# Differential q and k and the forgetting attention's gate with h's two halves as one 512-column stream

## The chip, the cores and the metric

The kernel runs on one core of one Trainium2 chip. The metric is the device time of one execution in microseconds (us). The kernel before took 937.58 us, the median of three runs (937.49 to 937.73). TensorE is called PE, VectorE DVE, ScalarE ACT, GpSimd POOL and SyncE, which starts the transfers of weights, SP.

## The reference, cut to what matters

Two layers of a streaming encoder on 256 rows of 1024 values. Each layer normalises its input to `h` and multiplies it by one wide matrix whose columns feed three branches: a forgetting attention (q, k, v, a gate `fg`), a state-space scan, and a differential attention (`dq`, `dk`, `dv`, a gate `dg`). Only these parts bear on the change:

```python
h = rmsnorm(x, norm_w)
proj = jnp.einsum('bld,de->ble', h, w_in)
(fq, fk, fv, ff, fg, sz, sxbc, sdt, dq, dk, dv, dg, mg) = jnp.split(proj, split_points, axis=-1)
...
y_a = o_a.transpose(0, 2, 1, 3).reshape(bsz, L, BRANCH_W) * jax.nn.silu(fg)
...
q = partial_rope(dq.reshape(bsz, L, DIFF_HEADS, 2, DIFF_HD), cos, sin).transpose(0, 2, 3, 1, 4)
k = partial_rope(dk.reshape(bsz, L, DIFF_HEADS, 2, DIFF_HD), cos, sin).transpose(0, 2, 3, 1, 4)
```

## The kernel before, in words

The precision is near float32, reached with fp32r matmuls: each operand is split into a high half (rounded to fp32r) and a low half (the rest), and of the four products three are summed, high by high, high by low and low by high.

**Weights.** They come in blocks of 512 columns, 34 to a layer, each in four units of 128 x 1024 (`load_chunk`). SP loads a unit (`raw`, four buffers), ACT casts it to the high half `whi` (L231), DVE subtracts to get the low half `wlo` (L232). Eight buffers of each kind hold two blocks.

**Two kinds of block.** In a B block (`bform`, L249) a piece of h is stationary and 512 columns of weights stream. In an A block (`aform`, L264) the weights are stationary and h, transposed, streams: 256 columns of its high or its low half. An A block has two halves of 48 matmuls, and each half fills one PSUM bank with two pieces of 128 outputs side by side. 14 blocks of a layer are A blocks: fq0, fk0, fg0, fq1, fk1, fg1 of the forgetting attention, four of the scan (sB, sC, sx0, sx1), and dq0, dk0, dq1, dk1 of the differential attention. Three banks (`pp`) take the sums of all blocks, three (`pq`) the small matmuls, two (`pt`) the transposes.

**h.** `make_h` normalises 128 rows at a time (`tt` is 0 or 1). `split_rows` transposes four pieces of 128 x 128 into one bank (L198), and `split_bank` takes them out two at a time: ACT copies the high half (L188), DVE subtracts for the low half (L189). The halves are four tiles each of 128 x 2 x 256; `at` picks one piece.

**What follows an A block.** `g_evac` (the gate): ACT takes a tanh from the bank and DVE makes the product, 512 columns each. `r_evac` (differential q and k): ACT copies 512 columns out (L792); the rotary step follows. `t_evac` (forgetting q and k) calls `split_q` or `split_k`, whose copies (L389, L394) and subtracts (L392) empty the bank.

**Beside the blocks** the attentions run as jobs: `scores` multiplies q by k (L406, L408) into a `pq` bank; DVE adds the mask and bias in one step (L411), ACT takes exponentials (L415). The bias of the forgetting attention reaches DVE by way of memory: `sc_cum` (L368, L369) is written to `scr` and read back as `sc`, and POOL masks it (L435).

**Order.** Each engine works in its own order, fixed ahead of the run by a list scheduler that the program uses; instructions with `URGENT` priority go first where they can. At the start a few weight casts are held behind h: the casts of the first block's units 1 to 3 are issued after the last copy and subtract of h's first 128 rows (`after=` in `load_chunk`), and its matmuls go by units (`EARLY`).

Of the kernel before, what the change touches and what calls it, by code (L numbers as in the profile page):

```python
# [24 lines left out]
KT = D // P  # L25
UNITS = 4
KU = KT // UNITS
# [69 lines left out]
def trunk(ctx: ExitStack, tc: tile.TileContext, x, norm_w, weights, small, vectors,  # L97
          final_norm_w, rope_t, out):
    nc = tc.nc
    V, S, G, PE = nc.vector, nc.scalar, nc.gpsimd, nc.tensor  # L100
# [6 lines left out]
    tp = ctx.enter_context(tc.tile_pool(name="tp", bufs=2))  # L107
    sm = ctx.enter_context(tc.tile_pool(name="sm", bufs=2))
    dr = ctx.enter_context(tc.tile_pool(name="dr", bufs=1, space=bass.MemoryType.DRAM))
    pp = ctx.enter_context(tc.tile_pool(name="pp", bufs=3, space=bass.MemoryType.PSUM))  # L110
    pq = ctx.enter_context(tc.tile_pool(name="pq", bufs=3, space=bass.MemoryType.PSUM))
    pt = ctx.enter_context(tc.tile_pool(name="pt", bufs=2, space=bass.MemoryType.PSUM))
# [3 lines left out]
    def a2(shape=None, dtype=F32):  # L116
        return ap.tile(shape or [P, 2, 256], dtype, name="a2")

    def rows():
        return [a2([P, 512]) for _ in range(2)]  # L120

    def halves():
        return tuple([a2(dtype=F32R) for _ in range(4)] for _ in range(2))

    def at(half, kt):
        return half[kt // 2][:, kt % 2, :]

    def bank(pool, name):
        return pool.tile([P, 512], F32, name=name)

    ident = const.tile([P, P], F32, name="ident")
# [47 lines left out]
    def rstd_of(ss, n, eps, width):  # L179
        r = sm.tile([P, 8], F32, name="rstd")  # L180
        V.tensor_scalar(out=r[:, 0:width], in0=ss, scalar1=1.0 / n, scalar2=eps,  # L181
                        op0=ALU.mult, op1=ALU.add)
        G.tensor_tensor(out=r[:, 0:width], in0=r[:, 0:width], in1=mhalf[:, 0:width], op=ALU.pow)  # L183
        return r

    def split_bank(ps, hi, lo, scale=None):
        if scale is None:
            return (S.copy(out=hi, in_=ps),  # L188
                    V.tensor_tensor(out=lo, in0=ps, in1=hi.bitcast(F32), op=ALU.subtract))  # L189
        else:  # L190
            S.activation(out=hi, in_=ps, func=AF.Copy, scale=scale)
            V.scalar_tensor_tensor(out=lo, in0=ps, scalar=scale, in1=hi.bitcast(F32),
                                   op0=ALU.mult, op1=ALU.subtract)

    def split_rows(src, hi, lo, tt, c):
        ps = bank(pt, "pt")
        for j in range(4):
            PE.transpose(ps[:, j * P:(j + 1) * P], src[:, j * P:(j + 1) * P], ident)  # L198
        ts = slice(tt * P, (tt + 1) * P)
        p4 = ps.rearrange("p (i j t) -> p i j t", i=2, t=P)  # L200
        for i in range(2):
            last = split_bank(p4[:, i], hi[2 * c + i][:, :, ts], lo[2 * c + i][:, :, ts])
        return last

    def norm_scale(ss):
        V.tensor_reduce(out=ss[:, 0:1], in_=ss, axis=AX.X, op=ALU.add)
        return rstd_of(ss[:, 0:1], D, EPS, 1)

    def norm_apply(xt, xs, r, wb, c):
        V.scalar_tensor_tensor(out=xs[c], in0=xt[c], scalar=r[:, 0:1], in1=wb[c],  # L210
                               op0=ALU.mult, op1=ALU.mult)

    chunks, _ = chunk_list()
# [39 lines left out]
    def aform(ch, act, jj):  # L253
        units, n = ch
        ahi, alo = act
        ps = bank(pp, "pp")
        for u in range(UNITS):
            whi, wlo = units[u]
            for k in range(KU):
                kt = u * KU + k  # L260
                for j in range(2):
                    c0 = (2 * jj + j) * P
                    for i, (w, a) in enumerate(((whi, ahi), (whi, alo), (wlo, ahi))):
                        PE.matmul(ps[:, j * T:(j + 1) * T], lhsT=w[:, k, c0:c0 + P], rhs=at(a, kt),  # L264
                                  start=(kt == 0 and j == 0 and i == 0), stop=(kt == KT - 1 and j == 1 and i == 2))
        return ps

    scr_x = dr.tile([2, P, D], F32, name="scr_x")
    L = [dict() for _ in range(DEPTH)]

    def make_h(l, tt, xt, xs, ss, gap):
        st = L[l]
        if tt == 0:
            st["hT"] = halves()
        with tc.high_priority(URGENT):
            r = norm_scale(ss)
            for c in range(2):
                norm_apply(xt, xs, r, st["nwb"], c)
        yield gap
        with tc.high_priority(URGENT):  # L280
            for c in range(2):
                st["split"] = split_rows(xs[c], st["hT"][0], st["hT"][1], tt, c)
        st[f"h{tt}"] = True

    def load_nwb(l):
# [11 lines left out]
    def start_job(gen, *args):  # L297
        jobs.append([gen(*args), slot[0]])
# [444 lines left out]
    def plan(l):  # L743
        st = L[l]
# [41 lines left out]
            return f  # L786

        def r_evac(key):
            def f(jj, ps):
                t = a2()  # L790
                st.setdefault("_" + key, []).append(t)
                S.copy(out=t, in_=ps.rearrange("p (a t) -> p a t", t=T))  # L792
                if jj == 1 and key[:2] == "dk":
                    start_job(rope, l, int(key[2]))
            return f

        def g_evac(key):
            def f(jj, ps):
                t = a2()
                p3 = ps.rearrange("p (a t) -> p a t", t=T)  # L800
                S.activation(out=t, in_=p3, func=AF.Tanh, scale=0.5)
                V.scalar_tensor_tensor(out=t, in0=t, scalar=1.0, in1=p3, op0=ALU.add, op1=ALU.mult)
                st[f"{key[0:2]}{2 * int(key[2]) + jj}"] = t
            return f

        def c_evac(key, j0):
            def f(jj, ps):
# [124 lines left out]
        for c in range(2):  # L932
            B(f"sz{c}", [gate_evac("sz", 512 * c, c == 1)])
        A("dq0", r_evac("dq0"), pre=start(diff))
        A("dk0", r_evac("dk0"))
        for c in range(2):
# [31 lines left out]
    def prefetch(n, after=None, behind=()):  # L968
        while queue and n > 0:
            l_, k_, _, off, m = queue.pop(0)  # L970
            loaded.append((l_, k_, load_chunk(off, m, after, behind)))
            n -= 1
# [16 lines left out]
    for tt in range(2):  # L989
        xs, ss = rows(), sm.tile([P, 4], F32, name="ss")  # L990
        with tc.high_priority(URGENT):
            for q in range(4):
                qs = slice(256 * (q % 2), 256 * (q % 2) + 256)
                a, b = xs[q // 2][:, qs], xt[tt][q // 2][:, qs]
                if q < ACTSQ[tt]:
                    S.activation(out=a, in_=b, func=AF.Square, accum_out=ss[:, q:q + 1])
                else:
                    V.tensor_tensor_reduce(out=a, in0=b, in1=b, scale=1.0,
                                           scalar=0.0, op0=ALU.mult, op1=ALU.add, accum_out=ss[:, q:q + 1])
        g = make_h(0, tt, xt[tt], xs, ss, 1)  # L1000
# [8 lines left out]
    for idx, it in enumerate(items):  # L1009
        if it["key"] == "dq0" and it["l"] == 0:  # L1010
            with tc.issue_after(L[0]["split"][0].ins), tc.issue_after(L[0]["split"][1].ins):
                load_params(1)
            nc.sync.dma_start(rot, rope_t)
        if it["pre"]:
            it["pre"]()
        l = it["l"]
        if it["wait"]:
            n = 0
            while it["wait"] not in L[l]:
                assert jobs  # L1020
                pump(100.0)
                n += 1
            if n > 1:
                print("forced", l, it["key"], n)
        prefetch(it["n"])
        got = [loaded.pop(0) for _ in range(it["n"])]
        assert got[0][:2] == (l, it["key"]), (got[0][:2], it["key"])
        if idx == 0:
            ch, act = got[0][2], it["act"]()
            it["evac"][0](0, bform(ch, act, 0, EARLY))  # L1030
            while "h1" not in L[0]:
                pump(BUDGET)
            it["evac"][0](1, bform(ch, act, 1))
            pump(BUDGET)
            got, it["evac"] = got[1:], it["evac"][1:]
            with tc.issue_after(L[0]["split"][0].ins), tc.issue_after(L[0]["split"][1].ins):
                load_params(0)
        for tt, pieces in enumerate(it.get("final", ())):
            while f"mT{tt}" not in L[l]:
                pump(100.0)  # L1040
            for c0, c1 in pieces:
                ps = bform(got[c0 // 512][2], it["act"](), tt, c0=c0 % 512, c1=c0 % 512 + c1 - c0)
                it["evac"](tt, c0, c1)(ps)
                pump(BUDGET)
        for s in range(0 if "final" in it else 2):
            for (_, _, ch), ev in zip(got, it["evac"]):
                if it["kind"] == "A":
                    ev(s, aform(ch, it["act"](), s))
                else:
                    while f"{it['flag']}{s}" not in L[l]:  # L1050
                        pump(100.0)
                    ev(s, bform(ch, it["act"](), s))
                pump(BUDGET)
# [27 lines left out]
```

## Time and profile before

| | |
|---|---|
| median of three runs | 937.58 us |
| profiled execution, its own time | 938.8 us |
| its span, first to last instruction | 937.1 us |
| PE busy | 924.8 us (99%) |
| DVE busy | 705.0 us (75%) |
| ACT busy | 588.0 us (63%) |
| mean granted clock of PE | 0.994 |

Busy is the time in which at least one instruction of the engine ran. Matmuls overlap in the profile: the time of a step is the distance from one start to the next, and a mean of 384 ns for a matmul is not its step. A timeline row gives its start, the time up to its last end, and in brackets the idle time of the engine ahead of it with what ended that.

### The profile page before, as it was taken

To read this page: it belongs to the slowest core of one execution; us is meant where nothing else is said; L and a number is where in the kernel's file an instruction comes from. 1 tells how busy PE (TensorE), PEld (TensorE's weight loads), DVE (VectorE), ACT (ScalarE), POOL (GpSimd) and SP (SyncE) were. 2 spreads that over 40 slices of the span, in tenths; PEclk is the share of its full clock that TensorE was granted. 3 is DMA by queue.
4 is the path that set the end of the run, shared out by engine and by line. 5 is a ranking of instruction groups with operands and counts; after the bars stand their busy time and mean duration, and the time that the engine had idled before them with its cause. 6 is when DMAs were issued, how large, how long until landed. Compare 5 with 4: busy or idle time off the path is not lost.

```text
span 937.1 us, 16550 instructions
## 1 busy us (share of the span) xinstructions
PE 924.8 (99%) x6012; PEld 828.5 (88%) x6012; DVE 705.0 (75%) x1472; ACT 588.0 (63%) x1115; POOL 56.9 (6%) x135
## 2 busy tenths in 40 slices
PE   7999999999999999999999999999999999999997
PEld 5999999988898988888889999998889899888886
DVE  5688888989667868764768789789877686787474
ACT  4668776655567768554546779666545695885441
POOL 2001200000010001100010111000001000010000
PEclk7999999999999999999999999999999999999999
DMA  6866735674555655555557674356646465554551
GB/s 227 266 214 209 222 102 169 206 241 137 179 184 175 191 173 180 175 157 198 191 174 258 222 225 151 125 180 207 209 150 199 155 203 174 189 180 153 186 179 45
DMA packets 60321, 172.48 MB, mean 184 GB/s; under 512 B 7312, under 2 KB 15824, under 8 KB 60240
## 3 DMA queue, kind: packets, MB, share of 16 engines
q1 hardware_dynamic: 59952, 170.91, 55.6%
q8 instruction: 47, 0.77, 0.3%
q10 hardware_dynamic: 288, 0.52, 0.1%
q14 instruction: 34, 0.28, 0.1%
HBM read 167.14 MB, written 2.16 MB: 181 GB/s over the span
## 4 chain that ended last, share of the span: by engine, by line
PE 96%; DMA 2%; DVE 1%; ACT 0%; SPq 0%; issue 0%; POOLq 0%; POOL 0%
PE pp L249 52%; PE pp L264 33%; PE pq L406 1%; PE pq L408 1%; PE pt L470 1%; PE pq L455 1%; PE pq L607 1%; DMA raw<-in_weights_dram 1%; PE pt L654 1%; PE pt L198 1%; PE pq L718 1%; PE pq L617 0%; DMA sc<-scr 0%; DMA scr<-sc_cum 0%; PE pt L549 0%; PE pt L725 0%
## 5 line engine op out<-in xcount | busy, mean ns | idle before, releaser
L249 PE MATMUL pp<-whi,a 128*128 128x512 f32 (+2 forms) x1488 | 452.6, 384 | 2.0 <-ACT a L188 1.2
L232 DVE TENSOR_TENSOR wlo<-raw,whi 128x1024 fp32r<-128x1024 f32 (+1 forms) x296 | 350.1, 1195 | 81.4 <-ACT whi L231 78.4
L231 ACT CAST whi<-raw 128x1024 fp32r<-128x1024 f32 (+1 forms) x296 | 301.9, 1028 | 126.6 <-PE pp L249 69.3
L264 PE MATMUL pp<-a,whi 128*128 128x256 f32 x1792 | 332.5, 284 | 0.0
L249 PEld LDWEIGHTS pp<-whi,a 128*128 128x128 f32 x1488 | 275.2, 189 | 55.4 <-ACT a L188 1.7
L249 PE MATMUL pp<-wlo,a 128*128 128x512 f32 (+2 forms) x744 | 282.9, 382 | 0.0
L264 PEld LDWEIGHTS pp<-a,whi 128*128 128x128 f32 x1792 | 281.2, 191 | 1.6 <-issue 0.9
L264 PE MATMUL pp<-a,wlo 128*128 128x256 f32 x896 | 254.7, 284 | 0.0
L264 PEld LDWEIGHTS pp<-a,wlo 128*128 128x128 f32 x896 | 171.2, 191 | 0.6 <-issue 0.2
L249 PEld LDWEIGHTS pp<-wlo,a 128*128 128x128 f32 x744 | 140.4, 189 | 25.8 <-DVE wlo L232 0.5
L494 DVE SCALAR_TENSOR_TENSOR a<-sw,pT,a 128x255 f32<-128x255 f32 (+2 forms) x96 | 42.0, 477 | 9.4 <-ACT a L491 9.2
L183 POOL TENSOR_TENSOR rstd<-rstd,mhalf 128x2 f32<-128x2 f32 (+2 forms) x24 | 18.5, 773 | 462.7 <-DVE rstd L181 462.7
L835 DVE SCALAR_TENSOR_TENSOR a<-a,pp 128x512 f32<-128x512 f32 x24 | 16.4, 683 | 22.3 <-PE pp L249 22.3
L188 ACT CAST a<-pt 128x256 fp32r<-128x256 f32 x32 | 11.5, 371 | 33.2 <-PE pt L198 26.4
L415 ACT ACTIVATE sc<-sc,nm 128x128 f32<-128x128 f32 (+1 forms) x64 | 28.5, 447 | 5.9 <-DVE nm L411 5.6
L391 POOL MEMSET a<- 64x256 f32 x64 | 18.8, 317 | 184.4 <-PE pq L408 80.9
L415 ACT ACTIVATE sc<-sc,dnm 128x128 f32<-128x128 f32 (+1 forms) x64 | 28.5, 449 | 0.6 <-DVE dnm L411 0.4
L406 PE MATMUL pq<-a,a 128*128 128x256 f32 (+1 forms) x128 | 27.0, 267 | 0.3 <-DVE nm L411 0.3
L435 POOL TENSOR_SCALAR_AFFINE_SELECT sc<-sc 128x256 f32<-128x256 f32 x32 | 16.3, 510 | 151.3 <-DMA sc<-scr 129.1
L411 DVE CUSTOM_DVE_ANT_0 sc<-pq,bmask 128x128 f32<-128x128 f32 (+1 forms) x64 | 20.2, 350 | 4.5 <-PE pq L408 4.5
L810 ACT COPY sw<-pp 128x512 f32<-128x512 f32 x16 | 9.3, 581 | 22.6 <-PE pp L264 17.0
L411 DVE CUSTOM_DVE_ANT_0 sc<-pq,sc 128x128 f32<-128x128 f32 (+1 forms) x64 | 19.7, 350 | 4.7 <-POOL sc L435 4.5
(168 smaller groups left out, 831.0 us busy)
## 6 DMA issues: line engine op xcount, KB each, us to landing
raw<-in_weights_dram SPq DMA_DIRECT2D x280, 512.0 KB, 4.5
raw<-in_weights_dram SPq DMA_DIRECT2D x16, 272.0 KB, 3.5
sc<-scr SPq DMA_DIRECT2D x16, 256.0 KB, 5.3
a<-scr SPq DMA_DIRECT2D x16, 256.0 KB, 6.1
a<-in_x_dram SPq DMA_DIRECT2D x8, 256.0 KB, 5.7
sc<-scr SPq DMA_DIRECT2D x16, 128.0 KB, 4.9
a<-in_norm_w_dram SPq DMA_DIRECT2D x4, 256.0 KB, 6.6
rp<-a SPq DMA_DIRECT2D x32, 32.0 KB, 3.2
```

Of the source, the lines that this page charges most:

```text
L183: G.tensor_tensor(out=r[:, 0:width], in0=r[:, 0:width], in1=mhalf[:, 0:width], op=ALU.pow)
L231: S.copy(out=hi, in_=raw)
L232: V.tensor_tensor(out=lo, in0=raw, in1=hi.bitcast(F32), op=ALU.subtract)
L249: PE.matmul(ps[:, 0:(c1 or n) - c0], lhsT=at(a, kt)[:, ts], rhs=w[:, k, c0:c1 or n], start=((u, k, i) == order[0]), stop=((u, k, i) == ord ...
L264: PE.matmul(ps[:, j * T:(j + 1) * T], lhsT=w[:, k, c0:c0 + P], rhs=at(a, kt), start=(kt == 0 and j == 0 and i == 0), stop=(kt == KT - 1 an ...
L391: G.memset(low[j][rest, i, :].bitcast(F32), 0.0)
L406: PE.matmul(ps[:, i * n:(i + 1) * n], lhsT=q[i][:, j, qs], rhs=k[i][:, j, 0:n], start=(i == 0), stop=False)
L411: V.tensor_tensor_reduce(out=sc[:, i, sl], in0=ps[:, i * n:(i + 1) * n], in1=bias(i)[:, sl], scale=-0.125, scalar=BIG, op0=ALU.add, op1=AL ...
L415: S.activation(out=sc[:, i, sl], in_=sc[:, i, sl], func=AF.Exp, scale=-1.0, bias=nm[:, i, t:t + 1], accum_out=rs[:, i, t:t + 1])
L435: G.affine_select(out=v, in_=v, pattern=[[0, 2], [-1, P]], compare_op=ALU.is_ge, fill=NEG, base=0, channel_multiplier=1)
L494: V.scalar_tensor_tensor(out=xc[:, s:T], in0=u[:, 0:T - s], scalar=pr["conv"](j, k), in1=xc[:, s:T], op0=ALU.mult, op1=ALU.add)
L835: V.scalar_tensor_tensor(out=t, in0=t, scalar=1.0, in1=ps, op0=ALU.add, op1=ALU.mult)
```

## The change

h is now eight tiles of 128 x 2 x 256, one for each 128 of the 1024 inputs: the high half in the first 256 columns, the low half behind it. `split_h` takes the place of `split_rows` for h and takes out one transposed piece at a time, as the two halves of a piece lie in one tile and two pieces don't. For fg0, fg1, dq0, dq1, dk0 and dk1 `wide_form` takes the place of `aform`: for each piece of 128 outputs, the high weights meet both halves of h in one matmul of 512 columns, and the low weights meet the high half in one of 256, which adds to the left half of the bank. A bank so holds one piece of 128 outputs, not two, and `folded` adds its two halves (an ACT copy of the right one, a DVE addition of the left) into a tile in SBUF ahead of what `g_evac` and `r_evac` did with the bank.

```diff
     def at(half, kt):
-        return half[kt // 2][:, kt % 2, :]
+        return half[kt] if len(half) == KT else half[kt // 2][:, kt % 2, :]
+
+    def side_by_side():
+        both = [a2(dtype=F32R) for _ in range(KT)]
+        return both, tuple([t[:, s, :] for t in both] for s in range(2))
...
+    def split_h(src, both, tt, c):
+        ps = bank(pt, "pt")
+        for j in range(4):
+            PE.transpose(ps[:, j * P:(j + 1) * P], src[:, j * P:(j + 1) * P], ident)
+        ts = slice(tt * P, (tt + 1) * P)
+        for j in range(4):
+            h = both[4 * c + j]
+            last = split_bank(ps[:, j * P:(j + 1) * P], h[:, 0, ts], h[:, 1, ts])
+        return last
...
+    def wide_form(ch, both, j):
+        units, n = ch
+        ps = bank(pp, "pp")
+        for u in range(UNITS):
+            whi, wlo = units[u]
+            for k in range(KU):
+                kt, cols = u * KU + k, slice(j * P, (j + 1) * P)
+                PE.matmul(ps, lhsT=whi[:, k, cols], rhs=both[kt], start=(kt == 0), stop=False)
+                PE.matmul(ps[:, 0:T], lhsT=wlo[:, k, cols], rhs=both[kt][:, 0, :],
+                          start=False, stop=(kt == KT - 1))
+        return ps
+
+    def folded(f, new):
+        pair = []
+
+        def g(j, ps):
+            if j % 2 == 0:
+                pair.append(new())
+            d = pair[-1][:, j % 2, :]
+            S.copy(out=d, in_=ps[:, T:2 * T])
+            V.tensor_tensor(out=d, in0=ps[:, 0:T], in1=d, op=ALU.add)
+            if j % 2:
+                f(j // 2, pair[-1])
+        return g
...
         def r_evac(key):
-            def f(jj, ps):
-                t = a2()
+            def f(jj, t):
                 st.setdefault("_" + key, []).append(t)
-                S.copy(out=t, in_=ps.rearrange("p (a t) -> p a t", t=T))
                 if jj == 1 and key[:2] == "dk":
                     start_job(rope, l, int(key[2]))
-            return f
+            return folded(f, a2)
...
                 if it["kind"] == "A":
-                    ev(s, aform(ch, it["act"](), s))
+                    if it["key"][:2] in ("dq", "dk", "fg"):
+                        for j in (2 * s, 2 * s + 1):
+                            ev(j, wide_form(ch, L[l]["both"], j))
+                    else:
+                        ev(s, aform(ch, it["act"](), s))
```

`g_evac` is wrapped in `folded` in the same way, with a scratch tile `sw`; its tanh and product then read that tile.

The scheduler sets a new order with the new instructions. ACT at the start, before: the cast of unit 0 of the first block, the copies of h's first 128 rows (`a_149` to `a_152`, two pieces each), two casts, then the squares for the second 128 rows.

```order
L231 CAST whi<-raw 128x1024 [waits DMAHW4_49]
L188 CAST a_149<-pt 128x2x128 [waits PE_49]
L188 CAST a_150<-pt 128x2x128 [waits DVE_49]
L188 CAST a_151<-pt 128x2x128 [waits PE_49]
L188 CAST a_152<-pt 128x2x128 [waits DVE_49]
L231 CAST whi<-raw 128x1024 [waits DMAHW5_49]
L231 CAST whi<-raw 128x1024 [waits DMAHW0_49]
L996 ACTIVATE a_229,ss<-a_107 128x256 [waits DMAHW6_49]
```

The same place on ACT now, from the fourth of eight copies of h (`a_149` to `a_156`, one piece each) on:

```order
L192 CAST a_152<-pt 128x128 [waits DVE_49]
L192 CAST a_153<-pt 128x128 [waits PE_49]
L192 CAST a_154<-pt 128x128 [waits DVE_49]
L192 CAST a_155<-pt 128x128 [waits DVE_49]
L192 CAST a_156<-pt 128x128 [waits DVE_49]
L1032 ACTIVATE a_237,ss<-a_107 128x256 [waits DMAHW6_49]
L1032 ACTIVATE a_237,ss<-a_107 128x256
L1032 ACTIVATE a_238,ss<-a_108 128x256 [waits DMAHW7_49]
L1032 ACTIVATE a_238,ss<-a_108 128x256
L245 CAST whi<-raw 128x1024 [waits DMAHW5_49]
```

The four squares (L1032, formerly L996) moved ahead of the cast of unit 1. PE in block fg0 of layer 0, before, where the scores (`pq`) stand among fg0's narrow matmuls; `a_149` and `a_153` are the two halves of h's first two pieces:

```order
L264 MATMUL pp<-a_149,wlo 128x256
L406 MATMUL pq<-a_839,a_616 128x256 [waits DVE_49,PE_49]
L406 MATMUL pq<-a_840,a_617 128x256
L408 MATMUL pq<-a_842,a_615 128x512
L264 MATMUL pp<-a_149,whi 128x256
L264 MATMUL pp<-a_153,whi 128x256
L264 MATMUL pp<-a_149,wlo 128x256
L406 MATMUL pq<-a_954,a_673 128x128 [waits DVE_49,PE_49,Activation_49]
```

The same place on PE now, from the end of fg0's second piece of 128 outputs on (L289 and L290 are the two matmuls of `wide_form`):

```order
L289 MATMUL pp<-a_156,whi 128x512
L290 MATMUL pp<-a_156,wlo 128x256
L445 MATMUL pq<-a_855,a_632 128x256 [waits DVE_49,PE_49]
L445 MATMUL pq<-a_856,a_633 128x256
L447 MATMUL pq<-a_858,a_631 128x512
L445 MATMUL pq<-a_970,a_689 128x128 [waits DVE_49,PE_49,Activation_49]
L289 MATMUL pp<-a_149,whi 128x512 [waits DVE_49]
L290 MATMUL pp<-a_149,wlo 128x256
```

The scores stand at the same step of the block, but fg0's third piece starts behind them with a new bank and a wait for DVE. DVE at that place now; `a2_972` and `a2_973` are what `split_k` subtracts for fk0's second half (L431, formerly L392), and L302 is the addition of `folded`:

```order
L450 ISA nm_871 128x1
L302 TENSOR_TENSOR sw_1077<-pp_1060,sw_1077 128x256 [waits Activation_49]
L450 ISA sc_719,nm_896<-pq_898,sc_719 128x128 [waits Pool_49]
L450 ISA nm_896 128x1
L450 ISA sc_719,nm_896<-pq_898,sc_719 128x128
L450 ISA nm_896 128x1
L431 TENSOR_TENSOR a2_972<-pp_921,a2_971 64x256 [waits Activation_49]
L431 TENSOR_TENSOR a2_973<-pp_921,a2_971 64x256
```

The order of the scores (L450, formerly L411) and of the subtracts is the one before, with the addition put in.

## Rows read from the trace of the kernel before

**Rows 1.** The page, parts 1, 4 and 5: busy, chain by engine, idle before casts.

```profile
PE 924.8 (99%) x6012; PEld 828.5 (88%) x6012; DVE 705.0 (75%) x1472; ACT 588.0 (63%) x1115; POOL 56.9 (6%) x135
...
PE 96%; DMA 2%; DVE 1%; ACT 0%; SPq 0%; issue 0%; POOLq 0%; POOL 0%
...
L231 ACT CAST whi<-raw 128x1024 fp32r<-128x1024 f32 (+1 forms) x296 | 301.9, 1028 | 126.6 <-PE pp L249 69.3
```

**Rows 2.** Chain of waits, 250 to 350 us: start us, us, what, times.

```profile
254.24 17.27 PE pp L264 x144
...
327.08 21.79 PE pp L249 x96
```

**Rows 3.** Timeline, ACT, start: start us, us, instruction, count, [idle before, releaser].

```profile
10.37 1.04 ACT L231 CAST whi<-raw 128x1024 fp32r<-128x1024 f32 x1 [6.10 <-DMA raw<-in_weights_dram]
...
13.04 0.65 ACT L188 CAST a<-pt 128x256 fp32r<-128x256 f32 x2 [1.35 <-DVE a L189]
...
14.50 1.99 ACT L231 CAST whi<-raw 128x1024 fp32r<-128x1024 f32 x2
16.40 0.42 ACT L996 ACTIVATE a<-a 128x256 f32<-128x256 f32 x1
...
18.01 2.21 ACT L231 CAST whi<-raw 128x1024 fp32r<-128x1024 f32 x3
```

**Rows 4.** Timeline, DVE, the same stretch.

```profile
12.59 0.42 DVE L189 TENSOR_TENSOR a<-pt,a 128x256 fp32r<-128x256 f32 x1
13.45 0.76 DVE L189 TENSOR_TENSOR a<-pt,a 128x256 fp32r<-128x256 f32 x2 [0.44 <-ACT a L188]
...
15.58 2.36 DVE L232 TENSOR_TENSOR wlo<-raw,whi 128x1024 fp32r<-128x1024 f32 x2 [0.52 <-ACT whi L231]
...
20.48 3.12 DVE L232 TENSOR_TENSOR wlo<-raw,whi 128x1024 fp32r<-128x1024 f32 x4
```

**Rows 5.** Timeline, PE, the same stretch.

```profile
15.60 2.07 PE L249 MATMUL pp<-whi,a 128*128 128x512 f32 x4 [0.80 <-ACT whi L231]
...
20.89 1.17 PE L249 MATMUL pp<-whi,a 128*128 128x512 f32 x4
```

**Rows 6.** Timeline, PE, block fg0 of layer 0.

```profile
66.53 0.40 PE L264 MATMUL pp<-a,whi 128*128 128x256 f32 x2
...
72.64 0.40 PE L406 MATMUL pq<-a,a 128*128 128x256 f32 x2
```

**Rows 7.** Timeline, DVE, the same stretch.

```profile
70.87 0.29 DVE L411 CUSTOM_DVE_ANT_0 sc<-pq,sc 128x128 f32<-128x128 f32 x1 [1.18 <-POOL sc L435]
...
73.11 0.77 DVE L392 TENSOR_TENSOR a<-pp,a 64x256 fp32r<-64x256 f32 x2
```

**Rows 8.** Timeline, PE, block fg0 of layer 1.

```profile
523.03 0.40 PE L264 MATMUL pp<-a,whi 128*128 128x256 f32 x2
...
529.94 0.47 PE L406 MATMUL pq<-a,a 128*128 128x256 f32 x2 [0.28 <-DVE nm L411]
```

**Rows 9.** Timeline, DVE, the same stretch.

```profile
529.28 0.29 DVE L411 CUSTOM_DVE_ANT_0 sc<-pq,sc 128x128 f32<-128x128 f32 x1 [2.72 <-POOL sc L435]
...
531.27 0.77 DVE L392 TENSOR_TENSOR a<-pp,a 64x256 fp32r<-64x256 f32 x2
```

**Rows 10.** Busy time by stretch around dq1 and dk1, layer 0; columns in the first line.

```profile
core 0: us, PE busy (x) PEld busy (x) DVE busy (x) ACT busy (x) POOL busy (x), PEclk, DMA share, GB/s
...
305.00:310.00 5.00, 5.00 (x42) 4.91 (x41) 4.96 (x22) 5.00 (x20) 0.00 (x0) 1.00 0.81 232
```

**Rows 11.** Groups by form, ACT: instruction xcount, busy us, mean ns, idle before.

```profile
L188 ACT CAST a<-pt 128x256 fp32r<-128x256 f32 x32 | 11.5, 371 | 33.2 <-PE pt L198 26.4 <-DVE a L189 6.7
...
L792 ACT COPY a<-pp 128x512 f32<-128x512 f32 x16 | 9.3, 580 | 16.4 <-PE pp L264 16.2
```

**Rows 12.** Groups by form, DVE.

```profile
L189 DVE TENSOR_TENSOR a<-pt,a 128x256 fp32r<-128x256 f32 x32 | 13.1, 420 | 10.3 <-ACT a L188 10.1
...
L802 DVE SCALAR_TENSOR_TENSOR a<-a,pp 128x512 f32<-128x512 f32 x8 | 5.4, 678 | 0.5 <-ACT a L801 0.5
```

More of the change, by code (lines that the diff above doesn't have):

```diff
@@ L273, in make_h @@
         if tt == 0:
-            st["hT"] = halves()
+            st["both"], st["hT"] = side_by_side()
         with tc.high_priority(URGENT):
@@ L281, in make_h @@
             for c in range(2):
-                st["split"] = split_rows(xs[c], st["hT"][0], st["hT"][1], tt, c)
+                st["split"] = split_h(xs[c], st["both"], tt, c)
         st[f"h{tt}"] = True
@@ L788, in r_evac, with f @@
         def r_evac(key):
-            def f(jj, ps):
-                t = a2()
+            def f(jj, t):
                 st.setdefault("_" + key, []).append(t)
-                S.copy(out=t, in_=ps.rearrange("p (a t) -> p a t", t=T))
                 if jj == 1 and key[:2] == "dk":
                     start_job(rope, l, int(key[2]))
-            return f
+            return folded(f, a2)
         def g_evac(key):
-            def f(jj, ps):
+            def f(jj, u):
                 t = a2()
-                p3 = ps.rearrange("p (a t) -> p a t", t=T)
-                S.activation(out=t, in_=p3, func=AF.Tanh, scale=0.5)
-                V.scalar_tensor_tensor(out=t, in0=t, scalar=1.0, in1=p3, op0=ALU.add, op1=ALU.mult)
+                S.activation(out=t, in_=u, func=AF.Tanh, scale=0.5)
+                V.scalar_tensor_tensor(out=t, in0=t, scalar=1.0, in1=u, op0=ALU.add, op1=ALU.mult)
                 st[f"{key[0:2]}{2 * int(key[2]) + jj}"] = t
-            return f
+            return folded(f, lambda: tp.tile([P, 2, T], F32, name="sw"))
         def c_evac(key, j0):
```

## The prediction

> **What bounds the kernel now.** I read the page's busy times first: PE is busy 99% of a span of 937.1 us, DVE 75%, ACT 63%, and the chain that ended last is 96% PE [rows 1]. So a change earns what it takes from PE's own steps and loses every wait that it puts in front of PE; work that it adds to ACT and DVE is free as long as PE doesn't wait for it. The casts of the weights show how much cover there is: most of ACT's idle time ahead of them, 69.3 of 126.6 us, ends when PE frees a weight buffer [rows 1], so over most of the span the weights are split before PE wants them. The chain of a stretch with the blocks concerned comes next, for the length of a step [rows 2], then the timelines of the three places where the new order puts something in front of PE: the start, and the block fg0 of both layers [rows 3 to 9].
>
> **The steps on PE.** 144 matmuls of 256 columns in a row took 17.27 us, 119.9 ns each; 96 of 512 columns took 21.79 us, 227.0 ns each [rows 2]. Twice the columns cost 107 ns more, so some 13 ns of each step don't go with the columns. Per weight tile a narrow block has three steps of 256 columns, 3 x 119.9 = 359.7 ns; a wide one has one of 512 and one of 256, 346.9 ns. The saving is 12.8 to 13.3 ns (the second if a step is taken as 120.0), 32 times a block, in 12 blocks (fg0, fg1, dq0, dq1, dk0, dk1 in two layers): 384 x 13.2 = 5.1 us. The 512-column row is of the other kind of block, where h is stationary and weights stream; I take it for the wide step. By columns alone nothing would be saved, and that is the one end; 5.1 us is the other. 5.1 it is, since it is the measured pair.
>
> The Trainium skill ("TensorE: Matmul & The Clock Gate", "Wait — 56ns, not 53.3ns?") speaks against this: it gives a fixed cost of some 2.5 ns for each back-to-back matmul at the full clock. By that rule the wide form would save an estimated 384 x 2.5 ns = 1.0 us and not 5.1. The steps of this trace, 119.9 and 227.0 ns, don't agree with it: what is left when the columns are taken off is five times that.
>
> **The start, +3.0 us.** The high and low halves of one 128-column piece now share a tile, so split_h makes eight pairs of copy and subtract for each half of the rows where split_rows made four of twice the width. ACT and DVE read the same bank in turn, and each copy waits for the subtract before it, as it did (the copies at 13.04 follow the subtract at 12.59, with an idle of 1.35 us that DVE ends [rows 3, 4]). A 256-column copy took 371 ns and a 512-column one 580 [rows 11], which makes 0.27 us for 128 columns; a subtract of 256 took 420 ns, a DVE operation of 512 columns 678 [rows 12], which makes 0.29; with two hand-overs of 0.035 us (12.59 plus 0.42 to 13.04) a pair lasts 0.63. The first subtract starts at 12.59 as before, behind wlo's first unit, and ends at 12.88. Six pairs more less 0.34, where the second bank's first copy runs beside a subtract, give 16.3, and the last copy ends at 16.6. By then ACT had cast two more units before, from 14.50 [rows 3]. In the new order the four squares of the second half of x come next, and took 18.01 - 16.40 = 1.61 us [rows 3]: 18.2. Then the cast of unit 1, 1.05 us: 19.3. PE, which got unit 1 at 15.60 [rows 5], gets it 3.7 us later and has nothing else.
>
> How much of it stays hangs on the clock. Four matmuls of 512 columns took 2.07 us at 15.60 and 1.17 us at 20.89 [rows 5]: PE was at the lower of its two levels until then, after about ten microseconds of work with two short gaps. If the clock rises at 20.9 whatever PE did, 1.6 us of the work that stood between 15.60 and 20.89 are done by then, and the other 3.7 us go in half the time: +1.9. If it rises as much later as PE starts, +3.7. The longer idle speaks for the later rise, so I take 3.0. DVE has its subtracts and the norm in front of unit 1's low half (before at 15.58, now behind the norm, which ends about where it did, 20.5 [rows 4]): 20.7 to 21.9, while PE has four matmuls and the eight transposes to do from 19.3 to 22. That adds nothing. A lag of the whole stream is not caught up later, as PE never waits for want of anything else.
>
> **The banks of fg0, +4.5 us.** A narrow block fills one bank with two pieces of 128 outputs and holds it for 48 steps, 5.76 us; a wide one fills a bank in 8 x 0.347 = 2.78 us, and there are three banks. fg0's third piece therefore needs the bank of fk0's second half 5.55 us after fg0 starts, and that one is emptied by split_k's subtract behind the first scores on DVE, which wait for a DMA and POOL. Layer 0: fg0's steps start at 66.53 [rows 6], two pieces end at 72.1, four score matmuls that stand between take 0.5: PE wants the bank at 72.6. Before, the subtract pair ran at 73.11 to 73.88 [rows 7]; now one fold, 0.42 us by the width of rows 12, stands ahead of it, partly in DVE's waits for POOL: 74.1. Wait 1.5 us. Layer 1: start 523.03 [rows 8], wanted at 529.1. The scores' DVE work started at 529.28, after 2.72 us of idle ended by POOL, and the pair ended at 531.27 + 0.77 = 532.04 [rows 9]; with the fold 532.4. Wait 3.3, of which 0.28 were there before [rows 8]: 3.0. Before, PE filled these microseconds with fg0's second half in a bank that had long been free. The bounds are nothing, if the bank comes in time, and 6 us, if the folds come in front in full. The wide block behind fk1 finds its banks free by about 1 us, by the same reckoning; I count nothing.
>
> **dq1 and dk1, +0.6 us.** Each wide block replaces two copies of 580 ns by four of 371 on ACT, +0.3 us, and adds four DVE additions of 420 ns, +1.7 us [rows 11, 12]. Over most blocks this lies beside PE. In 305 to 310 us, with forgetting attention's second group beside dq1, DVE was busy 4.96 and ACT 5.00 of 5.00 us [rows 10]. Two blocks add 3.4 us of DVE there and in the like stretch of layer 1. The casts of coming weights can give way, so I take 0.3 us for each layer; the ends are 0 and 2. The h of layer 1 is split while PE works at other things, and I count it at nothing.
>
> **The sum.** The profiled execution took 938.8 us: 938.8 - 5.1 + 3.0 + 4.5 + 0.6 = 941.8. The median of the runs is 937.58, 1.2 less; so 940.6.
>
> **Rivals.**
> (a) The bank comes in time. The place is fg0, the price the 4.5 us. If split_k's subtract runs before PE asks for the bank (72.6 and 529.1), only the start is left: -5.1 + 3.0, or 1.9 with the early clock, 934.4 to 935.5 us, faster. It decides from where both waits together fall under 0.2 us (1.3 with the early clock). For it: the margin is small in layer 0. Against it: the DMA that ends the wait doesn't hang on PE's new steps, and in layer 1 even the first scores were late.
> (b) Parts of it. The clock rises early (+1.9) and only layer 1's wait comes (+3.0): the sum is about 0, 937.4.
> (c) DVE is full. If the folds push the scores behind dq1 and dk1 by 2 us in each layer, +4 for +0.6: 944.0. For it rows 10; against it, the stretch is short and weight casts can wait.
> (d) The step goes by columns and nothing is saved: 945.7. By the trace's two lengths this is unlikely, but no row shows a 512-column step with weights stationary. The rule of the Trainium skill cited above would give 944.7.
>
> **How the numbers follow.** The forecast 0.42, (a) 0.20, (b) 0.17, (c) 0.14, (d) 0.07. Within 0.2% (1.9 us, about what a measurement here can tell from no change) lies (b): 0.17. Faster is (a), 0.20; slower is the rest, 0.63. The forecast's own range is 939 to 943. With half of (a), (b) and (c) the range is 935 to 945.
>
> **What would show it.** In the wide blocks, pairs of steps of 0.347 us (right) or 0.36 (d). At the start, PE idle of 4 to 4.5 us ended by ACT's cast of unit 1, and a second 512-column step length after about 23 us. In fg0, PE idle of 1.5 and 3 us ended by DVE's subtract of split_k; if it is under 0.3, (a). In dq1 and dk1, PE idle ended by DVE's score work. What would make the forecast wrong above all is that the bank is freed in time, or that PE's idle at the start is much shorter than 4 us.

## The result, and the profile after

The changed kernel takes 961.37 us (median of four runs) against 937.63: a ratio of 1.0249, 95% interval 1.0236 to 1.0262. It is slower by 23.7 us, where 3.0 were forecast, and far outside the range. Its profiled execution took 961.29 us with a span of 959.6. The spans of the two profiled executions differ by 22.5 us and not by 23.7, as the kernel before was profiled in an execution 1.2 us above its median.

Parts 1 and 4 of its page, busy times and the chain by engine (those of before are in [rows 1]):

```profile
PE 930.4 (97%) x5628; PEld 812.9 (85%) x5628; DVE 722.8 (75%) x1536; ACT 597.5 (62%) x1163; POOL 56.9 (6%) x135
...
PE 78%; DVE 7%; DMA 6%; ACT 5%; issue 3%; SPq 0%; POOLq 0%; DVEq 0%; ACTq 0%
```

PE's share of the chain fell from 96 to 78%: PE waits now, and DVE, ACT and DMA stand where it does. To see where, I set the two traces side by side. The B blocks have 2232 matmuls in both kernels (L249 before, L263 now), in the same order; the start of the n-th in one trace less its start in the other is the lag at that point. Lags in us, at the times of the kernel before:

| point (time before, us) | changed | start alone (e1) | narrow + fold (e6) | best (e12) |
|---|---|---|---|---|
| B blocks at the start done (38) | 3.2 | 2.6 | -0.6 | -0.4 |
| behind fg0, fg1 and the scan's blocks (179) | 2.3 | 2.7 | -0.6 | 0.2 |
| behind the scan's work (207) | 4.3 | 2.7 | 0.5 | 0.2 |
| behind dq0, dk0 (284) | 3.5 | 2.7 | 0.5 | -0.6 |
| behind dq1, dk1 (329) | 6.6 | 2.7 | 3.9 | -0.5 |
| inside the last B blocks of layer 0 (388) | 12.8 | 2.7 | 11.5 | 0.0 |
| layer 1, behind fg and scan (636) | 11.4 | 2.9 | 11.7 | -2.4 |
| behind dq0, dk0 (742) | 11.8 | 2.9 | 11.7 | -3.2 |
| behind dq1, dk1 (786) | 15.0 | 2.9 | 14.9 | -3.0 |
| inside the last B blocks (847) | 22.5 | 2.9 | 22.0 | -3.6 |

The start costs what was forecast, the blocks of fg themselves cost nothing, 2.0 and 1.2 us go behind the scan's work (near 207 and 673 us), and 20 us go in two places of each layer: 3 beside dq1 and dk1, 6 to 7.5 among the B blocks behind them. The lag also moves when small matmuls of the heads change their place: beside dq1 and dk1 36 of them now stand where 24 stood, 1.5 us more, and by the end of the layer's B blocks the same number is done in both kernels. So about half of the 3 us is work done earlier (PE's idle time there is 1.5 us), and that much more is lost behind; the sum of the two places stands.

**The start.** ACT and PE in the timeline of the changed kernel (rows 3 and 5 are theirs of before):

```profile
15.60 0.27 ACT L192 CAST a<-pt 128x128 fp32r<-128x128 f32 x1 [0.36 <-DVE a L193]
16.22 0.27 ACT L192 CAST a<-pt 128x128 fp32r<-128x128 f32 x1 [0.35 <-DVE a L193]
16.38 0.42 ACT L1032 ACTIVATE a<-a 128x256 f32<-128x256 f32 x1
...
17.99 3.47 ACT L245 CAST whi<-raw 128x1024 fp32r<-128x1024 f32 x4
```

```profile
19.07 2.07 PE L263 MATMUL pp<-whi,a 128*128 128x512 f32 x4 [3.34 <-ACT whi L245]
20.94 1.91 PE L212 MATMUL pt<-ident,a 128*128 128x128 f32 x8
22.50 1.20 PE L263 MATMUL pp<-wlo,a 128*128 128x512 f32 x2
23.50 1.71 PE L263 MATMUL pp<-whi,a 128*128 128x512 f32 x5
25.05 0.39 PE L263 MATMUL pp<-wlo,a 128*128 128x512 f32 x1
```

The last of eight copies starts at 16.22 (16.3 by the sum), 0.62 behind the one before; unit 1 reaches PE at 19.07, behind 3.34 us of idle (4 to 4.5 were named). The clock comes to the higher level between 23.50 and 25.05, where five matmuls of 512 columns take 1.55 us. The granted clock puts the rise at 24.3 us (0.50 in 22 to 24, 0.83 in 24 to 25, 1.00 behind), and in the kernel before at 21.0. So it came 3.3 us later, nearly as much as PE's start.

**fg0.** PE and DVE of the changed kernel, layer 0:

```profile
75.80 0.22 PE L445 MATMUL pq<-a,a 128*128 128x128 f32 x1
75.92 0.50 PE L289 MATMUL pp<-a,whi 128*128 128x512 f32 x1
```

```profile
75.44 0.42 DVE L302 TENSOR_TENSOR sw<-pp,sw 128x256 f32<-128x256 f32 x1
75.78 0.28 DVE L450 CUSTOM_DVE_ANT_0 sc<-pq,sc 128x128 f32<-128x128 f32 x1
...
76.31 0.77 DVE L431 TENSOR_TENSOR a<-pp,a 64x256 fp32r<-64x256 f32 x2
```

fg0's third piece starts at 75.92, when the fold of its first has just ended (75.44 + 0.42), and 1.2 us ahead of the end of split_k's subtracts (77.08), behind which I had put it. So the third piece can't have taken the bank of fk0's second half; by these times it took the one that came free first, its own block's.

**The steps.** In a quiet stretch a wide pair has the length that was forecast, 265.25 to 265.59, 0.347 us (the median of all pairs is 0.349):

```profile
265.25 0.39 PE L289 MATMUL pp<-a,whi 128*128 128x512 f32 x1
265.48 0.28 PE L290 MATMUL pp<-a,wlo 128*128 128x256 f32 x1
265.59 0.39 PE L289 MATMUL pp<-a,whi 128*128 128x512 f32 x1
```

Over dq0 and dk0 the lag falls by 0.74 us in either layer, where 64 groups at 13.2 ns make 0.85. The 2.5 ns of the Trainium skill ("TensorE: Matmul & The Clock Gate", "Wait — 56ns, not 53.3ns?") would make an estimated 0.16 us by its own figure; the trace doesn't agree with it.

**Behind dk1.** DVE of before and of the changed kernel, from the end of dk1 on. Before, dk1's last matmul started at 326.80, ACT's copy of the last half ended at 328.54, and the last two of the rotary step's eight transfers in (`rp<-a`), which read that copy, went out from 328.56 on:

```profile
333.45 0.75 DVE L679 STREAM_SHUFFLE sw<-rp 128x512 f32<-128x512 f32 x1
334.24 0.69 DVE L680 TENSOR_TENSOR sw<-sw,rot 128x512 f32<-128x512 f32 x1
334.85 0.69 DVE L681 TENSOR_TENSOR rp<-rp,rot 128x512 f32<-128x512 f32 x1
...
336.05 0.68 DVE L682 TENSOR_TENSOR rp<-rp,sw 128x512 f32<-128x512 f32 x1
```

```profile
332.58 4.63 DVE L246 TENSOR_TENSOR wlo<-raw,whi 128x1024 fp32r<-128x1024 f32 x4 [0.77 <-ACT whi L245]
337.13 0.41 DVE L302 TENSOR_TENSOR a<-pp,a 128x256 f32<-128x256 f32 x1
...
342.95 0.76 DVE L718 STREAM_SHUFFLE sw<-rp 128x512 f32<-128x512 f32 x1
343.59 1.21 DVE L246 TENSOR_TENSOR wlo<-raw,whi 128x1024 fp32r<-128x1024 f32 x1
344.71 0.69 DVE L719 TENSOR_TENSOR sw<-sw,rot 128x512 f32<-128x512 f32 x1
345.32 0.69 DVE L720 TENSOR_TENSOR rp<-rp,rot 128x512 f32<-128x512 f32 x1
345.92 2.36 DVE L246 TENSOR_TENSOR wlo<-raw,whi 128x1024 fp32r<-128x1024 f32 x2
348.19 0.69 DVE L721 TENSOR_TENSOR rp<-rp,sw 128x512 f32<-128x512 f32 x1
```

In the changed kernel dk1's last matmul starts at 333.33 and ACT's copy of its half ends at 335.66, behind four casts; but the addition stands behind four subtracts of the next weight block, starts at 337.13 and ends at 337.5. From there each further step of the chain meets another piece of that queue: three subtracts between the four rotary operations (5.9 us from the shuffle's start to the last's end, 3.3 before), and casts on ACT between the splits. The table counts from the start of dk1's last matmul in layer 0, in us:

| | before | changed | e6 | e10 | e11 | e13 | e14 |
|---|---|---|---|---|---|---|---|
| last `rp<-a` issued | 2.3 | 4.9 | 4.8 | 2.8 | 3.9 | 3.9 | 4.9 |
| rotary operations done on DVE | 9.9 | 15.6 | 15.5 | 10.3 | 12.1 | 12.3 | 16.0 |
| last `a<-rp` landed | 17.4 | 22.5 | 22.6 | 16.7 | 18.5 | 18.7 | 22.7 |
| split_k's first copy into the other half | 20.7 | 30.8 | 32.0 | 20.0 | 23.2 | 23.3 | 30.9 |
| first score on DVE | 29.9 | 36.8 | 36.9 | 27.5 | 29.3 | 29.6 | 34.9 |

A delay of 2.6 us at the head is 10 at the splits. In e11 and e13, whose addition is on POOL, 1.6 at the head is 2.5 and 2.6 there, and e13 has one subtract among the rotary operations, not three. So the delay at the head isn't the whole price: the order that the scheduler set behind it differs too, and no run separates the two. By the same count PE's first score came 6.3 us behind the last such copy before (29.3 and 23.0), and 1.2 in the changed kernel (33.3 and 32.1); now the scores come while DVE is full, and PE stands. PE in the changed kernel, with the clock of the same stretch below (columns in its first line):

```profile
370.76 0.47 PE L445 MATMUL pq<-a,a 128*128 128x256 f32 x2 [1.68 <-DVE dnm L450]
...
371.78 0.30 PE L445 MATMUL pq<-a,a 128*128 128x128 f32 x1 [0.31 <-DVE dnm L450]
373.33 0.55 PE L445 MATMUL pq<-a,a 128*128 128x256 f32 x1 [1.26 <-DVE dnm L450]
374.71 0.80 PE L763 MATMUL pt<-a,pT 128*128 128x128 f32 x2 [0.82 <-DVE a L772]
```

```profile
core 0: us, PE busy (x) PEld busy (x) DVE busy (x) ACT busy (x) POOL busy (x), PEclk, DMA share, GB/s
366.00:369.00 3.00, 3.00 (x18) 2.36 (x16) 1.34 (x3) 2.94 (x8) 1.31 (x3) 1.00 0.00 0
369.00:372.00 3.00, 1.01 (x5) 0.60 (x4) 3.00 (x12) 2.25 (x8) 0.00 (x0) 1.00 0.63 164
372.00:375.00 3.00, 0.92 (x3) 0.58 (x3) 3.00 (x14) 2.92 (x6) 0.00 (x0) 0.58 0.81 253
375.00:379.00 4.00, 4.00 (x16) 3.71 (x16) 3.54 (x11) 3.48 (x14) 0.00 (x0) 0.50 0.56 212
379.00:382.00 3.00, 3.00 (x14) 2.39 (x14) 2.66 (x12) 0.84 (x6) 1.54 (x2) 0.95 0.00 0
```

Idle 4.1 us between 369 and 375, DVE busy all the while; and with PE two thirds idle the granted clock fell to the lower level, where it stayed for four microseconds in which PE was busy again. 4.0 us at half speed are 2 us more. Together that is 6.1, and the lag rises by 6.2 here (6.6 to 12.8). With the small matmuls that had moved ahead the loss here is nearer 7.7; what is beyond 6.1 isn't broken down. Layer 1 has the same pattern: 4.1 us of idle ended by the same releasers, and a granted clock of 0.50 from 841 to 845 us. That the clock falls with little work and comes back with it is what the Trainium skill says ("TensorE: Matmul & The Clock Gate", "What's actually happening"); the trace agrees, 1.00 to 0.50 and back.

### The profile page after: what moved, and what is told of

It reads as the page before. It is cut to its first block, busy times and chain, and to the rows that moved or that the text cites. A ratio compares the mean times of both kernels' runs of the same rounds, so it can differ in the third digit from the quotient of the medians.

```text
span 959.6 us, 15901 instructions
## 1 busy us (share of the span) xinstructions
PE 930.4 (97%) x5628; PEld 812.9 (85%) x5628; DVE 722.8 (75%) x1536; ACT 597.5 (62%) x1163; POOL 56.9 (6%) x135
## 4 chain that ended last, share of the span: by engine, by line
PE 78%; DVE 7%; DMA 6%; ACT 5%; issue 3%; SPq 0%; POOLq 0%; DVEq 0%; ACTq 0%
PE pp L263 38%; PE pp L278 19%; PE pp L289 7%; PE pp L290 4%; DVE wlo L246 3%; DMA raw<-in_weights_dram 2%; ACT whi L245 2%; DMA rp<-a 1%; DVE sc L450 1%; PE pt L509 1%; PE pq L494 1%; DMA a<-rp 1%; PE pq L447 1%; ACT a L421 1%; ACT a L428 1%
## 5 line engine op out<-in xcount | busy, mean ns | idle before, releaser
L263 PE MATMUL pp<-whi,a 128*128 128x512 f32 (+2 forms) x1488 | 455.2, 386 | 8.0 <-ACT whi L245 3.3
L263 PEld LDWEIGHTS pp<-whi,a 128*128 128x128 f32 x1488 | 276.2, 190 | 62.5 <-ACT whi L245 4.1
L263 PE MATMUL pp<-wlo,a 128*128 128x512 f32 (+2 forms) x744 | 283.4, 383 | 0.0
L278 PE MATMUL pp<-a,whi 128*128 128x256 f32 x1024 | 190.9, 285 | 0.0
L263 PEld LDWEIGHTS pp<-wlo,a 128*128 128x128 f32 x744 | 140.9, 190 | 25.2
L278 PEld LDWEIGHTS pp<-a,whi 128*128 128x128 f32 x1024 | 160.4, 191 | 0.7 <-issue 0.6
L289 PE MATMUL pp<-a,whi 128*128 128x512 f32 x384 | 137.5, 398 | 3.0 <-ACT a L794 1.9
L290 PE MATMUL pp<-a,wlo 128*128 128x256 f32 x384 | 107.7, 281 | 0.0
L289 PEld LDWEIGHTS pp<-a,whi 128*128 128x128 f32 x384 | 72.1, 188 | 19.6 <-ACT a L794 2.5
L290 PEld LDWEIGHTS pp<-a,wlo 128*128 128x128 f32 x384 | 72.5, 189 | 0.2
L192 ACT CAST a<-pt 128x128 fp32r<-128x128 f32 (+1 forms) x48 | 14.0, 300 | 36.6 <-PE pt L202 25.4
L445 PEld LDWEIGHTS pq<-a,a 128*128 128x128 f32 x128 | 22.3, 190 | 10.6 <-issue 6.9
```

Source lines behind the costliest of these rows:

```text
L192: return (S.copy(out=hi, in_=ps), V.tensor_tensor(out=lo, in0=ps, in1=hi.bitcast(F32), op=ALU.subtract))
L263: PE.matmul(ps[:, 0:(c1 or n) - c0], lhsT=at(a, kt)[:, ts], rhs=w[:, k, c0:c1 or n], start=((u, k, i) == order[0]), stop=((u, k, i) == ord ...
L289: PE.matmul(ps, lhsT=whi[:, k, cols], rhs=both[kt], start=(kt == 0), stop=False)
L290: PE.matmul(ps[:, 0:T], lhsT=wlo[:, k, cols], rhs=both[kt][:, 0, :], start=False, stop=(kt == KT - 1))
L445: PE.matmul(ps[:, i * n:(i + 1) * n], lhsT=q[i][:, j, qs], rhs=k[i][:, j, 0:n], start=(i == 0), stop=False)
```

## The experiments

Theory F: the folds of dq and dk put DVE's queue into the chain from these blocks to the heads. Its rivals: B, banks wanted twice as often; W, the amount of DVE work; M, that it takes the wide matmuls too; S, that any new order upsets the late stages. Ratios are to the kernel before on the same chip. Of each edit the line that decides is shown; blocks that stay narrow keep the evacuation of before, and e9 and e11 to e15 have one to nine buffers fewer in the pool `ap`, where the new tiles stand.

**e1, the start alone.** All A blocks narrow, h as in the changed kernel:

```diff
-                    if it["key"][:2] in ("dq", "dk", "fg"):
+                    if False:
```

> h lies side by side and is taken out in eight pairs (split_h), but all A blocks stay narrow: the start alone. Theory F (the folds of dq and dk delay the rotary chain, and with it the differential attention's work, which then meets PE's last B blocks): only the start's 3.2 us are left, 940.8. Theory B (banks of one piece each make PE wait in dq1 and everything after follows from it): the same, 940.8. Theory S (the new order of the whole program, or a lag of 3 us, by itself upsets the late stages): 950 to 962.

942.65 us, 1.0048 (1.0033 to 1.0063), 1.9 us more than was expected. The lag is 2.6 at the start and 2.9 at the end, with no wait of PE behind the start: the start is one cost by itself, and S falls.

**e2, only fg wide.**

```diff
+                    if it["key"][:2] == "fg":
```

> As the changed kernel, but only fg0 and fg1 are wide; dq and dk are narrow. F and B: start +3.2, four blocks save 1.7 and the 0.28 of fg0's old wait, and nothing happens later: 939. S: 950 to 962. If fg0's third bank had a hidden price, over 941.

943.09 us, 1.0048 (1.0033 to 1.0063), as e1. It is over 941, but not for fg0's third bank: PE doesn't wait in fg0 of layer 0, and 0.45 us in layer 1. In layer 0 fg's blocks take 0.85 us off the lag, as they should, but 1.5 come back between 179 and 207 us, where PE waits once for a bank that ACT empties late (0.98 us): ACT's step stands behind a weight cast that waits 1.18 us for its transfer. In layer 1 0.4 go and 1.6 come back. The changed kernel shows 2.0 at the first place and 1.2 at the second. It is not fg's alone, as e3 and e6, where fg is narrow, show 0.9 and 1.1 at the first. Why the order there changes with a block so far ahead was not settled.

**e3, only dq and dk wide.**

```diff
+                    if it["key"][:2] in ("dq", "dk"):
```

> As the changed kernel, but only dq and dk are wide; fg is narrow. F and B: the whole loss comes from these blocks, so 961.4 plus the 2.0 us that fg's wide blocks save: 963. If fg's wide blocks push the late stages too: under 955.

960.84 us, 1.0242 (1.0226 to 1.0257): all of the late loss, 2 us under what was expected, since fg saved nothing on balance.

**e4, a bank for each piece.** The kernel before, with

```diff
+                S.copy(out=pair[-1][:, j % 2, :], in_=ps[:, 0:T])
```

for each piece of dq and dk in its own bank, three narrow matmuls to a weight tile.

> The kernel before, with h as it was and all blocks narrow, but in dq and dk each piece of 128 outputs has a bank of its own (half of it used) and is copied out by ACT alone, 256 columns at a time: a bank is wanted every 2.88 us, without any addition on DVE. B (the banks make PE wait): 4 to 8 us a layer lost, 946 to 954. F (it is the folds on DVE): no loss beyond four more ACT instructions a block, 937.6 to 939. S: anywhere.

938.01 us, 1.0003 (0.9993 to 1.0012). B falls, as far as banks go that ACT alone frees; those that a DVE instruction frees are in e10.

**e5, the folds first.**

```diff
+            with tc.high_priority(URGENT) if first else ExitStack():
```

> The changed kernel with one thing more: the two instructions of each fold in dq and dk (copy and addition) have URGENT priority, so that the scheduler sets them ahead of weight casts and scores. Theory F (the folds stand late in ACT's and DVE's order, the rotary chain starts late, and the heads' work meets the last B blocks): most of the 17 us of the late stages come back, 942 to 948. Theory W (it is not where the folds stand, but the amount of work that they add to two full engines): 956 to 962.

959.57 us, 1.0234 (1.0214 to 1.0255). It tells nothing: dk1's last fold still lets `rp<-a` go only 4.9 us behind the last matmul, as without priority. Priority didn't move the folds, so it didn't test where they stand.

**e6, the fold without the wide matmuls.** As e4, with

```diff
+                V.tensor_tensor(out=d, in0=ps[:, 0:T], in1=d, op=ALU.max)
```

> The kernel before, PE's blocks narrow, h as it was, one bank for each piece in dq and dk as in the run before of that kind, and after each ACT copy a DVE instruction that reads the bank and the copy (the larger of two equal numbers), so the fold's cost and place without its matmuls. F and W: the late stages lose what they lost, 17 to 19 us, 953 to 957. Theory M (the loss needs the wide matmuls too, which run PE ahead of the folds): under 945.

958.59 us, 1.0219 (1.0186 to 1.0251), a little over what F and W expected. PE's steps and h are those of before, and the loss is there, with PE's waits on the same releasers:

```profile
368.21 0.47 PE L419 MATMUL pq<-a,a 128*128 128x256 f32 x2 [0.78 <-DVE dnm L424]
...
370.36 0.78 PE L419 MATMUL pq<-a,a 128*128 128x128 f32 x2 [1.45 <-DVE dnm L424]
...
373.04 0.80 PE L737 MATMUL pt<-a,pT 128*128 128x128 f32 x2 [1.90 <-DVE a L746]
```

M falls: the fold does it alone.

**e7 and e8, one pair of blocks wide.** `WIDE = ("dq0", "dk0")`, and `("dq1", "dk1")`.

> The changed kernel with only dq0 and dk0 wide (in both layers). F: the first rotary chain is late, dq1's wait for dv1's bank and for the first heads' scores stays, 3 us a layer, less 0.85 saved: start 4 + 2 x 2.2, 945 to 948; the second chain is in time. If the 6 to 8 us a layer beside the last blocks come from the first pair: 955 or more.

> The changed kernel with only dq1 and dk1 wide. F: the second chain is late, 6.3 and 7.5 us are lost beside the last B blocks, start 4, saved 1.7: 952 to 956. If all hangs on the first pair: 940 to 943.

943.1 us, 1.0057 (1.0037 to 1.0076), and 955.23 us, 1.0179 (1.0159 to 1.0199). The second pair makes most of the loss. e7 lost less beside dq1 than expected (1.7 us in either layer, not 3).

**e10, the same work beside the chain.** As e6, but DVE writes where nobody reads:

```diff
-                V.tensor_tensor(out=d, in0=ps[:, 0:T], in1=d, op=ALU.max)
+                x = tp.tile([P, T], mybir.dt.bfloat16, name="unused", bufs=1)
+                V.tensor_tensor(out=x, in0=ps[:, 0:T], in1=d, op=ALU.max)
```

> As the narrow kernel with the fold's two instructions in dq and dk, but the DVE instruction writes into a scratch tile that nobody reads, and the rotary step takes ACT's copy. DVE has the same work to do and the bank waits for it all the same, but the rotary chain doesn't. Theory F (what costs is that the chain from dq and dk to the heads gets DVE's queue in front of it): 937.5 to 941. Theory W (the amount of DVE work in a full stretch): 953 to 959, as with the result used.

937.99 us, 1.000 (0.999 to 1.001). The DVE instruction has the same place in both: dk1's last one starts 3.67 us behind the last matmul in e6 and in e10. So the same work and the same bank releases cost 20 us less: W falls, B with it, and what costs is that the rotary step waits for the fold.

**e11, the fold on POOL; e12, that and h in pairs; e9, h in pairs alone.**

```diff
-            S.copy(out=d, in_=ps[:, T:2 * T])
-            V.tensor_tensor(out=d, in0=ps[:, 0:T], in1=d, op=ALU.add)
+            u = tp.tile([P, 2, T], F32, name="fd", bufs=1)
+            S.copy(out=u, in_=ps.rearrange("p (a t) -> p a t", t=T))
+            G.tensor_tensor(out=d, in0=u[:, 0, :], in1=u[:, 1, :], op=ALU.add)
```

```diff
+        both = [hp.tile([P, 2, 2, T], F32R, name="hh") for _ in range(4)]
+        return both, tuple([t[:, :, s, :] for t in both] for s in range(2))
```

> The changed kernel with the fold taken off DVE: ACT copies the whole bank into SBUF, 512 columns, and POOL, which is busy 6%, adds the two halves. F: the start's 3 to 4 us stay, the chain has ACT's copy and a POOL addition without a queue, 5.1 us saved on PE: 937 to 944. W: the same, or worse by ACT's 0.2 us a piece. If what costs is a second step in the chain at all, on whatever engine: 950 and more.

> As the one before, and h lies in four tiles of two pieces, each with its high and its low half side by side, so that it is taken out of the bank 256 columns at a time as in the kernel before while the 512 columns stay in one run. If the start's loss comes from the eight pairs: 3 to 4 us below the one before; if F holds as well, 933 to 940.

> The kernel before with only h's tiles changed as in the run above (four tiles of two pieces with both halves), all blocks narrow. If the start's loss comes from the eight pairs of the changed kernel and not from where h lies: 937.5, within 1. If reading h from tiles of twice the length costs PE anything, over 939.

e11: 940.26 us, 1.0026 (1.0016 to 1.0036). e12: 936.03 us, 0.9977 (0.9968 to 0.9987), the only one faster than the kernel before by more than the noise. e9: 937.02 us, 0.9992 (0.9983 to 1.0002). A POOL addition lasts twice as long as DVE's, 835 ns, and yet it is the faster way, as nothing stands in front of it (in e12 dk1's last one starts at 328.99, and ACT's copy ended at 328.91):

```profile
L294 POOL TENSOR_TENSOR a<-fd 128x256 f32<-128x256 f32 x32 | 26.7, 835 | 90.4 <-ACT fd L293 90.4
```

The 4.2 us between e11 and e12 are the eight pairs of the start: the lag at 38 us is 3.6 in e11 and -0.4 in e12, 4.0 apart, and so it is at the end (0.5 and -3.5). In e12 PE gets unit 1 at 15.54.

```profile
15.54 2.07 PE L254 MATMUL pp<-whi,hh 128*128 128x512 f32 x4 [1.03 <-ACT whi L236]
```

The clock at the start isn't the same in every execution. e9's nine runs took 935.64 to 939.08 us with mean granted clocks of 0.999 to 0.992. Its profiled one, the fastest, had a granted clock of 1.00 from 10 to 20 us, where the kernel before had 0.50 from 11 to 21, and its B blocks lead those of the kernel before by 3.2 us from there to the end.

**e13 and e14, dk1's fold alone.** The changed kernel with only dk1's folds on POOL (e13, shown), and with all but dk1's (e14, `key != "dk1"`).

```diff
-            return folded(f, a2)
+            return folded(f, a2, key == "dk1")
```

> The changed kernel, all folds on DVE but those of dk1, which ACT copies whole and POOL adds. If dk1's fold at the head of the second rotary chain makes the late loss: 13 to 14 us less than the changed kernel, 946 to 949, with the first pair's 3 us a layer left. If the folds' work on DVE makes it: 956 or more.

> The reverse: all folds on POOL but those of dk1, which stay on DVE. If dk1's fold makes the late loss: 940 plus 12 to 14, 951 to 955. If it is the sum of the folds: 940 to 944.

945.01 us, 1.0074 (1.0055 to 1.0094), and 955.97 us, 1.0191 (1.0171 to 1.021). dk1's folds, at the head of the second rotary chain, make 16 us: 961.37 less 945.01, and 955.97 less e11's 940.26. Each run lies a microsecond outside what was expected for that answer. In e14 DVE shows the changed kernel's pattern, subtracts of weights ahead of the fold and between the rotary steps:

```profile
329.80 2.36 DVE L246 TENSOR_TENSOR wlo<-raw,whi 128x1024 fp32r<-128x1024 f32 x2
332.07 0.42 DVE L307 TENSOR_TENSOR a<-pp,a 128x256 f32<-128x256 f32 x1
...
338.39 0.76 DVE L723 STREAM_SHUFFLE sw<-rp 128x512 f32<-128x512 f32 x1
339.04 1.21 DVE L246 TENSOR_TENSOR wlo<-raw,whi 128x1024 fp32r<-128x1024 f32 x1
```

**e15, the scan's blocks wide too,** on top of e12.

```diff
+                    if it["key"][:2] in ("dq", "dk", "fg", "sB", "sC", "sx"):
```

> The fastest kernel so far (h in pairs, folds on POOL) with the scan's four A blocks a layer (sB, sC, sx0, sx1) wide as well, their two halves added by POOL into the tile that ACT filled alone before. Eight blocks of 32 groups at 13.2 ns: 3.4 us less than 936.0, 932.6, if ACT's second copy for each tile and POOL's additions stay beside PE; if the convolution behind them is late by POOL's 0.85 us a piece and DVE's queue, 936 or more.

949.62 us, 1.0122 (1.0106 to 1.0138): a trade of the same kind, and lost. PE waits 1.42 us in the scan's blocks for ACT's copies and up to 2.41 behind them, the granted clock falls to 0.59 in 208 to 212 us, and the steps' 3.4 us are given back five times over:

```profile
160.18 0.50 PE L280 MATMUL pp<-hh,whi 128*128 128x512 f32 x1 [1.42 <-ACT fd L293]
...
207.81 0.76 PE L254 MATMUL pp<-whi,a 128*128 128x512 f32 x1 [2.41 <-ACT a L811]
```

## Why the prediction was wrong

- **The steps, -5.1: right, a little large.** 0.347 us a pair where it is quiet, 0.349 in the median, and a fall of the lag by 0.74 us over two blocks where 0.85 were counted.
- **The start, +3.0: right in its working, a little small.** 3.2 in the lag of the changed kernel, between the two ends given (1.9 and 3.7), and the clock rose later, as was taken; but e1 measured 4.5 (3.1 to 5.9) and e12 against e11 4.2, above the upper end. One reading was off: PE was not at the lower level from the first on, as the granted clock was 1.00 up to 10.8 us in the kernel before.
- **The banks of fg0, +4.5: wrong, it was nothing.** I had the banks go round in turn. By the times the third piece got the bank of the block's first piece, freed by its fold. Rival (a) had the right price for another reason: it wanted split_k's subtract done before PE asks, and that ended 1.2 us behind PE's start.
- **dq1 and dk1, +0.6: the step that failed.** It was sized at 0 to 2 us a layer as work beside PE: so many additions against DVE's free time, with casts that can give way. It measured 10 and 11 us in the two layers (by the lag 3.9 and 4.0 beside the blocks, 6.2 and 7.5 behind), and the amount of work was not the fault, as e10 shows: the same work costs nothing. The step asked how much DVE has to do, not who waits for the fold. Ahead of the change `r_evac` gave its tile to the rotary step after one ACT copy; now the tile passes DVE's queue, where the work of the next weight block did not give way: four 1.2 us subtracts stand ahead of the addition. I followed the bank behind each fold, and not the tile; the rotary chain, with transfers in and out and three queues to pass, stands nowhere in the prediction. Rival (c) named the place, but as fullness, and priced it at 2 us a layer. What stays open is how much of the loss hangs on the order that the scheduler set behind the late tile: e5 was to move the folds and didn't.
- **No term for the clock.** PE's waits were priced as their own length. With enough of them in one place the clock fell, and a third of the 6 us there is half speed.

The numbers add up: -5.1 and +3.2 for steps and start, 3.9 and 4.0 beside dq1 and dk1 (the lag's rise of 3.0 and 3.2 with the saving of 0.85 that it hides), 6.2 and 7.5 behind them, and some 3 us near 207 and 673 us make 22.7, against 22.5 in the span. The step saving stands there as it was forecast.

## What to carry to other kernels

When a copy out of a bank gets a second instruction on another engine, ask who reads its result, and follow that chain through every queue to the engine that ends last; an operation that is free as work can be dear as a link. Here the link was cheap on the engine with no queue, though the addition took twice as long there. A few ns saved on each matmul pay only if all that they ask of the engines beside it stays out of such chains: of 5.1 us on PE, 1.7 were left in the best form (937.73 less 936.03).

## What the runs showed of the hardware that was not expected

A PE that waited in short pieces (4.1 of 6 us, none longer than 1.7) dropped to the lower clock level, 1.00 to 0.50, and was still there for four busy microseconds. At the start, two kernels alike but for h's tiles ran at a granted clock of 0.50 (the kernel before, 11 to 21 us) and 1.00 (e9, 10 to 20 us) in the executions that were profiled. An addition of two tiles of 256 columns took POOL 835 ns, where DVE took 0.41 to 0.43 us with one of the two in a bank.
